# Gates in column tiles, softplus and scan moved, first weights in four pieces from two queues, first norm's squares from a token-major copy of x

## The chip, the cores and the metric

The kernel runs on one core of one Trainium2 chip. The metric is device time in microseconds (us) of one execution, lower is better. A core has TensorE (PE in the profile; PEld is its weight load), VectorE (DVE), ScalarE (ACT), GpSimd (POOL) and SyncE (SP), each with its own queue of instructions, and 16 DMA engines that all transfers share. TensorE writes to PSUM, from which the other engines read.

## The reference

A trunk of two layers over 256 tokens of width 2048, in fp32. Layer 0 runs two recurrences side by side, HGRN2 and RG-LRU; layer 1 is an mLSTM with input and forget gates. Each layer is followed by a gated per-layer embedding (PLE). Cut to what the change touches:

```python
def rmsnorm(x, g):
    return x * lax.rsqrt(jnp.mean(x * x, axis=-1, keepdims=True) + EPS) * g

def rg_lru(xc, w_r, b_r, w_i, b_i, lam):            # layer 0, second half
    r  = sigmoid(blocks(xc) @ w_r + b_r)            # 8 blocks of 128
    ig = sigmoid(blocks(xc) @ w_i + b_i)
    log_a = -8.0 * r * softplus(-lam)
    a = exp(log_a)
    u = sqrt(-expm1(2.0 * log_a)) * (ig * xc)
    return associative_scan(h[t] = a[t] * h[t-1] + u[t])

h = x
for i in range(2):
    hn = rmsnorm(h, norm[i])
    u = hn @ w_in[i]                                # projections of the layer
    ...                                             # mixers
    # layer 1: li = u[gates i] + b_i, lf = log_sigmoid(u[gates f] + b_f), 8 heads each
    h = h + mixed @ w_out[i]
    h = h + rmsnorm(p[i] @ ple_w[i], ple_norm[i]) * silu(h @ ple_gate_w[i])
return rmsnorm(h, final_norm)
```

## The kernel before

**Products.** A fp32 product is made of three matmuls of fp32r halves: a weight is loaded raw (128x1024, 512 KB, five buffers, on SyncE's queue), ScalarE casts it to `whi` (L124, four buffers), VectorE subtracts to get `wlo` (L125, four buffers). Activations are kept as pairs `ahl` of the same kind. `block` multiplies feature-major: 16 matmuls of 128x512 on `whi` (L155), then 16 of 128x256 on `wlo` (L161). `project_tok` multiplies token-major: three matmuls of 128x512 per tile (L196 on `whi`, L197 on `wlo`, L198 on `whi`), in four quarters `kq` of the contraction. `mm3` (L144 to L146) does the same for the small PLE product.

**What sets the order.** Python code issues the instructions in the order of the main line: one projection after another. Beside it run "lanes": generators that yield between steps. `pump()`, called between the two passes of `block` and after the first half of each quarter of `project_tok`, steps every lane once, and what the lanes issue is put behind the last weight instructions of TensorE, ScalarE and VectorE. `drain` runs a lane to its end on the spot. `high_priority` puts an instruction ahead in its engine's queue. Each engine then works strictly through its own row of instructions, so what stands behind a long or a waiting instruction waits too.

**The stages.** First `ple(load_p(0), ...)` multiplies the per-layer embedding: `praw` is loaded and cast (L139), `pw` is loaded, its first half in two pieces of 256 KB. Then `i_proj(0)`, a token-major projection whose quarter `kq` calls `load_x(kq)`: it loads a quarter `xq` of the transposed x, splits it with the gain (L277 on ScalarE, L278 on VectorE), and squares it on ScalarE (L272; the first quarter pair L269); the squares are added up in `acc` on GpSimd and, for the last two pairs, on VectorE (L273). After the fourth quarter the lane "norm" folds `acc` on GpSimd, `rs_tok` sums it over partitions with four small matmul records (L223), `newton` makes the inverse root, and `to_free` (L233 on VectorE, a diagonal `dg`; L236 on TensorE) spreads it over the partitions. The end of `i_proj` scales by `rt`.

Then follow `i_proj(1)`, projections for f and q, the lane "att" (HGRN2; among its matmuls L556, L625 and L643, each of which fills a PSUM bank `mx` that VectorE or ScalarE reads), the projections for `xb` with the convolution `xc` (L738), and the lane "rg", which runs `rg_lru` for the two halves r = 0 and 1: gate matmuls (L704), sigmoids (L708), tanh and exp (L714, L715), squares, `tt` (L721), square root (L723), product (L724), a memset (L725) and the scan (L726, one instruction of 128x1024 on VectorE). They run in the pumps of the two `gate_tok` projections on `ez`. After these, `drain("rg")` runs what is left of the lane, then come four `gate_mul`. PSUM `mx` has three banks.

In layer 1, four token-major projections `ov` are followed by the gates: `gr` is loaded, each half of the contraction gets a zeroed 128x1024 `whi` buffer into which the eight columns of each gate are written as a high and a low half (columns 0, 32, 64 and 96 of each 128), and 32 matmuls (L839) with 128 columns and 256 tokens make the 16 rows. The lane "mix" then runs `gate_stats`: copy the high rows, add the low rows, scale, bias, then logs and two scans; `split8` (L244, L245) splits the running maximum `Mx` in two 8-row tiles and L876 transposes two of the results. `mix(j)`, for four pairs of heads, spreads a row of `Mx` over 128 partitions with `spread`, two matmuls for each head (L252, L253).

**The preparation** `derive` makes the constants of both recurrences on ScalarE and VectorE in the lane "par", among them the softplus of `lam` (L489, L490), all within the first projections.

Of the kernel before, what the change touches and what calls it, by code (L numbers as in the profile page):

```python
# [39 lines left out]
NCST = 128 + 32 + 16 + 2 * 48 + 256  # L40
# [3 lines left out]
def trunk(ctx: ExitStack, tc: tile.TileContext, a, out):  # L44
# [58 lines left out]
    tri2 = cst[:, c0:c0 + 256]  # L103

# [8 lines left out]
    def load_weights(src, pieces=1):  # L113
        parts = []
        for hf in range(2):
# [123 lines left out]
    def split8(x, name):  # L239

        n = x.shape[0]
        hi = tp.tile([8, T], F32R, name=name + "h", tag="s8h", bufs=1)[0:n, :]
        lo = tp.tile([8, T], F32R, name=name + "l", tag="s8l", bufs=1)[0:n, :]
        v.tensor_copy(hi, x)  # L244
        v.tensor_tensor(out=lo, in0=x, in1=hi.bitcast(F32), op=ALU.subtract)  # L245
        return hi, lo

    def spread(o, parts, h):

        n = parts[0].shape[0]  # L250
        w = identr[0:n, h:h + 1].to_broadcast([n, P])
        te.matmul(o, w, parts[0], start=True, stop=False)  # L252
        te.matmul(o, w, parts[1], start=False, stop=True)  # L253
# [48 lines left out]
    def load_p(i):  # L302
        praw = tp.tile([P, 512], F32, name="praw", tag="hn", bufs=3)
        sy.dma_start(out=praw, in_=a["pT"][i])
        return split_act(praw, "p")

    def ple(pact, pool, between):
        pls = []
        for b in range(2):
            parts = load_weights(a["pw"][b], 2 if b == 0 else 1)  # L310
            if b == 1:
                between()
            for j in range(4):
# [150 lines left out]
    def derive():  # L464
        sy.dma_start(out=cst, in_=a["cst"])
# [13 lines left out]

        lam = pall("lam")  # L480
# [14 lines left out]
        v.tensor_scalar(spm8, sp, -8.0, None, op0=ALU.mult)  # L495

# [3 lines left out]
    with m0_scope:  # L500
# [191 lines left out]
        def rg_lru(r, xc):  # L692
# [5 lines left out]
            yield  # L698
            for j in range(2):
# [24 lines left out]
            v.tensor_tensor(out=it, in0=it, in1=tt, op=ALU.mult)  # L724
            v.memset(av.rearrange("p (c t) -> p c t", t=T)[:, :, 0:1], 0.0)  # L725
# [15 lines left out]
        vts = [i_proj(0), i_proj(1)]  # L741
# [44 lines left out]
    v.tensor_copy(identr, ident[0:8, 0:8])  # L786
# [3 lines left out]
    with tc.tile_pool(name="m1", bufs=2) as m1:  # L790
# [35 lines left out]
        for hf in range(2):  # L826
            wt = wp.tile([P, 1024], F32R, name="whi", tag="whi")
# [405 lines left out]
```

## Time and profile before

| | us |
|---|---|
| time, median of 3 runs | 1080.57 (1078.49 to 1080.72) |
| the profiled execution's own time | 1082.2 |
| its span, first to last instruction | 1080.4 |
| PE busy | 1060.6 (98%), 6042 instructions |
| DVE busy | 748.2 (69%), 1087 |
| ACT busy | 579.9 (54%), 852 |
| POOL busy | 131.6 (12%), 103 |
| DMA | 200.26 MB, 185 GB/s in the mean |

The mean granted clock of TensorE is 0.996 of full speed. Row by row, a group line of the profile names a line of the code, an engine, the operation, out<-in with partitions x elements, the count, the busy time and the idle time before it with its releaser. A timeline line has the start, the busy time, the engine, the line, the operation and, in brackets, the idle time before it and what ended it. TensorE's records overlap: a matmul is recorded as busy for longer than the distance to the next start. A full-fp32 matmul (not split) leaves two records.

### The profile page before, as it was taken

Reading aid. Unit: us, or ns where it says so; the run is one execution under the profiler, and the core shown is the slowest. Engines: PE = TensorE matmul, PEld = TensorE weight load, DVE = VectorE, ACT = ScalarE, POOL = GpSimd, SP = SyncE. Lnnn points to the kernel's source line nnn. Section 1 sums busy time; section 2 is a strip of 40 time slices with the busy share of each in tenths; the row PEclk is TensorE's granted clock in tenths of the full one; section 3 lists DMA queues with packets and bytes.
Section 4 is the critical chain, followed back from the end, with each engine's and each line's share of the span. In section 5 each row is a group of like instructions: output and inputs, shape, how many; then the busy total and the mean of one; then the engine's idle time right before and its main releaser. Section 6 shows DMA issues by size and latency. Waiting matters only on the chain.

```text
span 1080.4 us, 15904 instructions
## 1 busy us (share of the span) xinstructions
PE 1060.6 (98%) x6042; PEld 912.9 (84%) x6042; DVE 748.2 (69%) x1087; ACT 579.9 (54%) x852; POOL 131.6 (12%) x103
## 2 busy tenths in 40 slices
PE   7999999999999999999999999999999999999996
PEld 7788888878888888888888888888888888888886
DVE  6958987987777556777544877764456677655665
ACT  7565545857654435556444766554444466434543
POOL 2143542521000000112000000000000005000111
PEclk9999999999999999999999999999999999999999
DMA  8555553533755555555554544445555765554542
GB/s 317 202 205 177 175 186 134 195 131 126 277 197 183 193 195 185 190 189 184 194 195 158 193 156 157 156 166 195 194 190 187 239 217 180 192 191 173 185 176 79
DMA packets 55948, 200.26 MB, mean 185 GB/s; under 512 B 6208, under 2 KB 6464, under 8 KB 55872
## 3 DMA queue, kind: packets, MB, share of 16 engines
q1 hardware_dynamic: 54720, 195.06, 51.5%
q0 software_dynamic: 1152, 4.19, 1.1%
q8 instruction: 47, 0.77, 0.3%
q14 instruction: 29, 0.24, 0.1%
HBM read 197.13 MB, written 2.10 MB: 184 GB/s over the span
## 4 chain that ended last, share of the span: by engine, by line
PE 92%; DVE 4%; ACT 1%; issue 1%; DMA 0%; SPq 0%; DVEq 0%; ACTq 0%
PE mm L155 32%; PE mm L161 17%; PE mm L196 12%; PE mm L197 12%; PE mm L198 12%; DVE wlo L125 2%; DVE ahl L278 1%; PE mm L1082 1%; PE mm L1081 1%; PE mm L1080 1%; PE nu L918 1%; DMA raw<-in_pw_dram 0%; PE mx L444 0%; PE mx L556 0%; ACT whi L124 0%
## 5 line engine op out<-in xcount | busy, mean ns | idle before, releaser
L125 DVE TENSOR_TENSOR wlo<-raw,whi 128x1024 fp32r<-128x1024 f32 (+1 forms) x361 | 455.5, 1286 | 237.1 <-ACT whi L124 136.6
L124 ACT CAST whi<-raw 128x1024 fp32r<-128x1024 f32 (+1 forms) x361 | 377.1, 1048 | 330.3 <-PE mm L155 158.0
L155 PE MATMUL mm<-ahl,whi 128*128 128x512 f32 x1536 | 367.2, 391 | 0.0
L155 PEld LDWEIGHTS mm<-ahl,whi 128*128 128x128 f32 x1536 | 282.1, 188 | 56.1 <-DVE ahl L278 0.7
L196 PE MATMUL mm<-whi,ahl 128*128 128x512 f32 x608 | 239.4, 394 | 0.0
L197 PE MATMUL mm<-wlo,ahl 128*128 128x512 f32 x608 | 236.8, 390 | 1.1 <-DVE wlo L125 1.1
L198 PE MATMUL mm<-whi,ahl 128*128 128x512 f32 x608 | 236.8, 390 | 0.0
L161 PE MATMUL mm<-ahl,wlo 128*128 128x256 f32 x1536 | 202.1, 284 | 0.0
L161 PEld LDWEIGHTS mm<-ahl,wlo 128*128 128x128 f32 x1536 | 195.5, 191 | 6.7
L197 PEld LDWEIGHTS mm<-wlo,ahl 128*128 128x128 f32 x608 | 114.3, 188 | 24.5 <-DVE wlo L125 1.5
L198 PEld LDWEIGHTS mm<-whi,ahl 128*128 128x128 f32 x608 | 114.1, 188 | 23.9
L196 PEld LDWEIGHTS mm<-whi,ahl 128*128 128x128 f32 x608 | 114.3, 188 | 23.4
L167 ACT COPY sm<-mm 128x256 f32<-128x256 f32 x64 | 23.6, 369 | 41.5 <-PE mm L161 41.5
L273 POOL TENSOR_TENSOR acc<-acc,sq 128x512 f32<-128x512 f32 x11 | 17.4, 1580 | 215.4 <-ACT sq L272 215.2
L980 POOL DMA_DIRECT2D row<-in_rows_dram x4 | 2.1, 537 | 285.0 <-DVE u L970 264.9
L168 DVE TENSOR_TENSOR mg<-mm,sm 128x256 f32<-128x256 f32 x64 | 26.6, 415 | 0.1
L803 DVE SCALAR_TENSOR_TENSOR qk<-mg,prm,qk 128x255 f32<-128x255 f32 (+2 forms) x48 | 21.3, 480 | 6.8 <-ACT qk L800 6.5
L1068 POOL TENSOR_TENSOR pl<-pl,row 128x512 f32<-128x512 f32 x6 | 9.2, 1533 | 134.5 <-ACT sq L1052 134.5
L1080 PE MATMUL mm<-whi,ahl 128*128 128x256 f32 x64 | 18.3, 285 | 0.0
L1082 PE MATMUL mm<-whi,ahl 128*128 128x256 f32 x64 | 18.1, 283 | 0.0
L1081 PE MATMUL mm<-wlo,ahl 128*128 128x256 f32 x64 | 18.1, 283 | 0.0
L178 DVE TENSOR_TENSOR mg<-mg,hrs 128x512 f32<-128x512 f32 (+1 forms) x25 | 17.7, 707 | 0.5
(292 smaller groups left out, 825.9 us busy)
## 6 DMA issues: line engine op xcount, KB each, us to landing
raw<-in_ew_dram SPq DMA_DIRECT2D x64, 512.0 KB, 4.3
raw<-in_g_dram SPq DMA_DIRECT2D x56, 512.0 KB, 3.7
raw<-in_eo_dram SPq DMA_DIRECT2D x32, 512.0 KB, 4.0
raw<-in_ov_dram SPq DMA_DIRECT2D x32, 512.0 KB, 3.7
raw<-in_oqk_dram SPq DMA_DIRECT2D x32, 512.0 KB, 4.1
raw<-in_oog_dram SPq DMA_DIRECT2D x32, 512.0 KB, 3.8
raw<-in_oz_dram SPq DMA_DIRECT2D x32, 512.0 KB, 3.8
raw<-in_oo_dram SPq DMA_DIRECT2D x32, 512.0 KB, 3.9
```

The source lines that it names most:

```text
L124: last["act"] = s.copy(h, r).ins
L125: last["dve"] = v.tensor_tensor(out=l, in0=r, in1=h.bitcast(F32), op=ALU.subtract).ins
L155: last["pe"] = te.matmul(ps, parts[k // 8][0][:, c:c + P], act[k // 2][2][:, (k % 2) * 512:(k % 2 + 1) * 512], start=(k == 0), stop=False).ins
L161: last["pe"] = te.matmul(ps[:, T:2 * T], parts[k // 8][1][:, c:c + P], act[k // 2][0][:, k % 2], start=False, stop=(k == KT - 1)).ins
L167: s.copy(small, ps[:, T:2 * T])
L168: v.tensor_tensor(out=dst, in0=ps[:, 0:T], in1=small, op=ALU.add)
L196: te.matmul(ps[hf], xh, wh, start=(k == 0), stop=False)
L197: te.matmul(ps[hf], xh, wl, start=False, stop=False)
L198: last["pe"] = te.matmul(ps[hf], xl, wh, start=False, stop=(k == KT - 1)).ins
L1080: te.matmul(ps[hf], xh, wh, start=(k == 0), stop=False)
L1081: te.matmul(ps[hf], xh, wl, start=False, stop=False)
L1082: last["pe"] = te.matmul(ps[hf], xl, wh, start=False, stop=(k == KT - 1)).ins
```

## The change

Five edits.

1. **First weights.** `load_weights` can alternate between queues, and the first half of the first `pw` is loaded in four pieces of 128 KB, alternating between ScalarE's and SyncE's queue. The cast of `praw` and the PLE matmuls get an explicit place.
2. **First norm.** A token-major copy of x is a new input. Four loads `xt` of 128x1024 are issued on SyncE's queue, two in `load_x(2)` and `load_x(3)`, two behind `i_proj(0)`. Four ScalarE activations square them and sum along the row (`accum_out`), VectorE adds two columns, and the inverse root follows. The eight squares, the adds on GpSimd and VectorE, the fold and the four L223 records of that norm go.
3. **Softplus.** The part of `derive` on `lam` becomes a lane of its own, `decay`, started after `i_proj(0)`, in four pieces. The load of the constants `cst` waits one pump longer.
4. **Scan.** `rg_lru` yields once more before the gate matmuls when r is 1, and once more before the memset and the scan. `drain("rg")` is replaced by stepping the lane until the half that `gate_mul` needs is there.
5. **Gates.** A 128x16x32 tile `wt` holds the gate columns times the gain `on` in fp32. 16 fp32 matmuls (32 columns, 256 tokens) take the raw `hq` and go to four column tiles of one PSUM bank, by k mod 4. ScalarE copies the bank to `gm`, and one fp32 matmul with a constant matrix `gsum` adds the four tiles into 40 rows, one pump later, in `gate_stats`, which then reads PSUM directly. `split_rows` puts both halves of `Mx` into one 40-row tile, and `spread` is one matmul per head.

```diff
-                sy.dma_start(out=r, in_=src[:, hf * 1024 + c:hf * 1024 + c + n])
+                queues[(hf * 1024 + c) // n % len(queues)].dma_start(out=r, in_=src[:, hf * 1024 + c:hf * 1024 + c + n])
...
+    def split_rows(x):
+
+        both = tp.tile([40, T], F32R, name="s8", tag="s8", bufs=1)
+        v.memset(both.bitcast(F32), 0.0)
+        v.tensor_copy(both[0:8], x)
+        v.tensor_tensor(out=both[32:40], in0=x, in1=both[0:8].bitcast(F32), op=ALU.subtract)
+        return both
+
+    def spread(o, both, h):
+
+        te.matmul(o, identr[:, h:h + 1].to_broadcast([40, P]), both, start=True, stop=True)
...
-            parts = load_weights(a["pw"][b], 2 if b == 0 else 1)
+            parts = load_weights(a["pw"][b], *((4, (s, sy)) if b == 0 else ()))
...
+    def load_xt(i):
+        sy.dma_start(out=xt[i], in_=a["x"][i // 2 * P:(i // 2 + 1) * P, i % 2 * 1024:(i % 2 + 1) * 1024])
+
+    def x_norm():
+
+        for i in range(4):
+            s.activation(xt[i], xt[i], AF.Square, accum_out=xss[:, i % 2, i // 2:i // 2 + 1])
+            if i < 3:
+                yield
+        y = xss[:, 0]
+        v.tensor_tensor(out=y, in0=y, in1=xss[:, 1], op=ALU.add)
+        v.tensor_scalar(y, y, 1.0 / D, EPS, op0=ALU.mult, op1=ALU.add)
+        yield from spread_norm(rsqrt_cols(y), 0)
...
             acth.append(gained(pair_of(xq, j), "en", j))
-            add_square(gp if j < 6 else v, acc, pair_of(xq, j), j == 0)
-        if i == 3:
-            start("norm", finish_norm([folded(acc)], 0))
+        if i >= 2:
+            load_xt(i - 2)
+        if i == 2:
+            start("norm", x_norm())
...
             yield
+            if r:
+                yield
             for j in range(2):
                 for w, (dst, bias) in enumerate(((av, "bbr"), (it, "bbi"))):
...
             v.tensor_tensor(out=it, in0=it, in1=tt, op=ALU.mult)
+            yield
             v.memset(av.rearrange("p (c t) -> p c t", t=T)[:, :, 0:1], 0.0)
             v.tensor_tensor_scan(tt, av, it, 0.0, op0=ALU.mult, op1=ALU.add)
...
-        vts = [i_proj(0), i_proj(1)]
+        vts = [i_proj(0)]
+        start("par", decay())
+        vts.append(i_proj(1))
...
-        drain("rg")
         for j in range(4):
             if j == 2:
                 drain("att")
+            if j % 2 == 0:
+                while ("h", j // 2) not in res:
+                    step("rg")
...
+        wt = m1.tile([P, KT, 32], F32, name="wt", tag="wt", bufs=1)
+        gp.memset(wt, 0.0)
+        v.tensor_tensor(out=wt[:, :, 0:16], in0=gr, in1=pall("on").unsqueeze(2).to_broadcast([P, KT, 16]), op=ALU.mult)
         ps = pm.tile([P, 512], F32, name="mm", tag="mm")
...
+        for k in range(KT):
+            c = 32 * (k % 4)
+            te.matmul(ps[c:c + 32, 0:T], wt[:, k], pair_of(hq, k // 2)[:, (k % 2) * T:(k % 2 + 1) * T],
+                      start=(k < 4), stop=(k >= KT - 4))
+        gm = m1.tile([P, T], F32, name="gm", bufs=1)
+        s.copy(gm, ps[:, 0:T])
...
+        def gate_stats():
+            yield
+            ps = px.tile([P, 512], F32, name="mx", tag="mx")
+            te.matmul(ps[0:40, 0:T], gsum, gm, start=True, stop=True)
...
-                s.copy(x, ps[c:c + 8, 0:T])
-                v.tensor_tensor(out=x, in0=x, in1=ps[64 + c:72 + c, 0:T], op=ALU.add)
-                v.tensor_tensor(out=x, in0=x, in1=norm["rs"][0:8], op=ALU.mult)
+                v.tensor_tensor(out=x, in0=ps[c:c + 8, 0:T], in1=norm["rs"][c:c + 8], op=ALU.mult)
```

Lines of the kernel after lie a little lower: L124 and L125 become L126 and L127, L155 and L161 become L157 and L163, L196 to L198 become L198 to L200, L236 becomes L238, L643 becomes L671, L704 becomes L737, L726 becomes L760, L839 becomes L872.

On ScalarE, at the start of the program, the row of instructions was this; `raw` and `whi` are the first PLE weights, `praw` the embedding, `pl` the product.

```order
L139 ACT_TABLE_LOAD
L139 CAST ahl<-praw 128x2x256
L124 CAST whi<-raw 128x512 x2
L124 CAST whi<-raw 128x1024 x2
L324 COPY pl<-mm 128x512
```

And now:

```order
L124 DMA raw<-in_pw_dram 128x256 x2
L126 ACT_TABLE_LOAD
L126 CAST whi<-raw 128x256
L141 CAST ahl<-praw 128x2x256
L126 CAST whi<-raw 128x256 x3
L126 CAST whi<-raw 128x1024 x2
L326 COPY pl<-mm 128x512
```

Two loads are issued ahead of everything, the first weight piece is cast ahead of the embedding, and there are four casts of half the width.

On VectorE, around the r = 0 scan during the first `ez` projection, the row before was this; `xc` is the convolution, `f` and `A` belong to HGRN2, the two wide ones on `tt` and `it` to RG-LRU (the scan is printed under the name of another operation).

```order
L125 TENSOR_TENSOR wlo<-raw,whi 128x1024 x2
L738 SCALAR_TENSOR_TENSOR xc<-mg,prm,xc 128x255 x2
L738 SCALAR_TENSOR_TENSOR xc<-mg,prm,xc 128x254 x2
L738 SCALAR_TENSOR_TENSOR xc<-mg,prm,xc 128x253 x2
L726 SCALAR_TENSOR_TENSOR tt<-av,it 128x1024
L631 TENSOR_TENSOR f<-f,tot_2480 128x8x64
L125 TENSOR_TENSOR wlo<-raw,whi 128x1024
L638 COPY A<-mx 64x8x64
L125 TENSOR_TENSOR wlo<-raw,whi 128x1024
L716 TENSOR_TENSOR it<-it,xc 128x1024
L125 TENSOR_TENSOR wlo<-raw,whi 128x1024 x2
```

And now:

```order
L127 TENSOR_TENSOR wlo<-raw,whi 128x1024 x2
L772 SCALAR_TENSOR_TENSOR xc<-mg,prm,xc 128x255 x2
L772 SCALAR_TENSOR_TENSOR xc<-mg,prm,xc 128x254 x2
L772 SCALAR_TENSOR_TENSOR xc<-mg,prm,xc 128x253 x2
L127 TENSOR_TENSOR wlo<-raw,whi 128x1024
L659 TENSOR_TENSOR f<-f,tot_2470 128x8x64
L127 TENSOR_TENSOR wlo<-raw,whi 128x1024
L666 COPY A<-mx 64x8x64
L760 SCALAR_TENSOR_TENSOR tt<-av,it 128x1024
L127 TENSOR_TENSOR wlo<-raw,whi 128x1024 x2
L480 SCALAR_TENSOR_TENSOR u<-u,mm 128x512
```

The scan (L726, now L760) moved from ahead of `f` and the copy to `A` to behind both, and the product `it` with `xc` of the half r = 1 (L716) no longer stands here.

On TensorE, around the gates of layer 1, between the last `ov` projection and the first blocks of `oqk`, the row was this; `li`, `Bc` and the `Mx` halves are results of `gate_stats`.

```order
L198 MATMUL mm<-whi,ahl 128x512
L839 MATMUL mm<-ahl,whi 128x256 x32
L155 MATMUL mm<-ahl,whi 128x512 x16
...
L876 MATMUL mx<-cst,li 128x8 x2
L876 MATMUL mx<-cst,Bc 128x8 x2
...
L252 MATMUL mx<-Mxh,identr 128x256
L253 MATMUL mx<-Mxl,identr 128x256
L252 MATMUL mx<-Mxh,identr 128x256
L253 MATMUL mx<-Mxl,identr 128x256
```

And now:

```order
L200 MATMUL mm<-whi,ahl 128x512
L872 MATMUL mm<-hq,wt 32x256 x16
L157 MATMUL mm<-ahl,whi 128x512 x16
...
L888 MATMUL mx<-gm,cst 40x256
...
L912 MATMUL mx<-cst,li 128x8 x2
L912 MATMUL mx<-cst,Bc 128x8 x2
L251 MATMUL mx<-s_5769,identr 128x256 x2
```

16 matmuls of 32 columns stand for 32 of 128, one matmul for the sum is added one pass later, and the two spread matmuls now follow directly on the transposes.

More of the change, by code (lines that the diff above doesn't have):

```diff
@@ L39 @@
 NPRM = _o
[L40 removed]
+NCST = 128 + 32 + 16 + 2 * 48 + 256 + 40
 @with_exitstack
@@ L103, in trunk @@
     tri2 = cst[:, c0:c0 + 256]
+    c0 += 256
+    gsum = cst[:, c0:c0 + 40]
     def pc(name, i=0, n=None):
@@ L110, in pall, with load_weights @@
         return pc(name, 0, PRM[name][1])
-    def load_weights(src, pieces=1):
+    def load_weights(src, pieces=1, queues=(sy,)):
         parts = []
@@ L237, in to_free @@
         return st[:, 0:T]
[L239 to L253, printed above, removed]
+    def split_rows(x):
[6 more added lines that the diff above has]
+        te.matmul(o, identr[:, h:h + 1].to_broadcast([40, P]), both, start=True, stop=True)
     def folded(acc, *more):
@@ L304, in load_p @@
         sy.dma_start(out=praw, in_=a["pT"][i])
-        return split_act(praw, "p")
+        with tc.high_priority(offset=0 if i else 800):
+            return split_act(praw, "p")
     def ple(pact, pool, between):
@@ L319, in ple @@
                         c = ((j % 2) * 4 + jj * 2 + k) * P
-                        mm3(ps[:, jj * T:(jj + 1) * T], hi[:, c:c + P], lo[:, c:c + P], pact, k, k == 0, k == 1)
+                        with ExitStack() as behind:
+                            if "pe" in last:
+                                behind.enter_context(tc.issue_after(last["pe"]))
+                            mm3(ps[:, jj * T:(jj + 1) * T], hi[:, c:c + P], lo[:, c:c + P], pact, k, k == 0, k == 1)
                 if j % 2:
@@ L401, in trunk @@
     pls = ple(load_p(0), p0, lambda: sy.dma_start(out=prm, in_=a["prm"]))
-    identr = cp.tile([8, 8], F32R, name="identr")
-    acc = cp.tile([P, 512], F32, name="acc", tag="acc")
+    identr = cp.tile([40, 8], F32R, name="identr")
     acth = []
+    xt = [hp.tile([P, 1024], F32, name="xt", tag="h") for _ in range(4)]
+    xss = cp.tile([P, 2, 2], F32, name="xss")
+    def load_xt(i):
[9 more added lines that the diff above has]
+        yield from spread_norm(rsqrt_cols(y), 0)
     def load_x(i):
@@ L423, in finish_norm, with spread_norm @@
             yield
-        norm["rt"] = rs_tok(accs)
+        yield from spread_norm(rs_tok(accs), lag)
+    def spread_norm(rt, lag):
+        norm["rt"] = rt
         yield
@@ L478, in derive, with decay @@
         yield
+    def decay():
         lam = pall("lam")
@@ L650, in i_proj @@
             ps = project_tok(a["ei"], g, acth, None if g else load_x)
-            vt = hp.tile([P, 1024], F32, name="vt", tag="h")
+            if g == 0:
+                for i in (2, 3):
+                    load_xt(i)
             while "rt" not in norm:
                 step("norm")
+            vt = hp.tile([P, 1024], F32, name="vt", tag="h")
             for hf in range(2):
@@ L783, in trunk @@
     l0.close()
-    v.tensor_copy(identr, ident[0:8, 0:8])
+    v.memset(identr.bitcast(F32), 0.0)
+    for c in (0, 32):
+        v.tensor_copy(identr[c:c + 8], ident[0:8, 0:8])
     norm.clear()
@@ L824, in trunk @@
         sy.dma_start(out=gr, in_=a["ogf"])
+        wt = m1.tile([P, KT, 32], F32, name="wt", tag="wt", bufs=1)
+        gp.memset(wt, 0.0)
+        v.tensor_tensor(out=wt[:, :, 0:16], in0=gr, in1=pall("on").unsqueeze(2).to_broadcast([P, KT, 16]), op=ALU.mult)
         ps = pm.tile([P, 512], F32, name="mm", tag="mm")
-        for hf in range(2):
-            wt = wp.tile([P, 1024], F32R, name="whi", tag="whi")
-            gp.memset(wt.bitcast(F32), 0.0)
-            w3 = wt.rearrange("p (k c) -> p k c", c=P)
-            f3 = wt.bitcast(F32).rearrange("p (k c) -> p k c", c=P)
-            for w in range(2):
-                src = gr[:, hf * 8:(hf + 1) * 8, w * 8:(w + 1) * 8]
-                c = w * 32
-                s.copy(w3[:, :, c:c + 8], src)
-                v.tensor_tensor(out=w3[:, :, 64 + c:72 + c], in0=src, in1=f3[:, :, c:c + 8], op=ALU.subtract)
-            for kk in range(8):
-                k = hf * 8 + kk
-                for i, x in enumerate(acth[k // 2][0:2]):
-                    te.matmul(ps[:, 0:T], wt[:, kk * P:(kk + 1) * P], x[:, k % 2],
-                              start=(k == i == 0), stop=(k == KT - 1 and i == 1))
+        for k in range(KT):
[4 more added lines that the diff above has]
+        s.copy(gm, ps[:, 0:T])
         def t8(name):
@@ L877, in gate_stats @@
             v.tensor_copy(aT, px_[:, 0:32])
-        start("mix", gate_stats(ps))
+        start("mix", gate_stats())
         SC = 0.25 * 128.0 ** -0.5
@@ L1159, in _const @@
     c[:, o:o + P] = np.where(si <= np.arange(P)[None, :], 0.0, -1e30)
+    o += 256
+    for h in range(8):
+        c[:, o + h] = si[:, 0] % 32 == h
+        c[:, o + 32 + h] = si[:, 0] % 32 == 8 + h
     return c
```

9 lines of the change are left out of this document (7 added, 2 removed).

## The prediction

> **What bounds the kernel now.** I read the first part of the page, then its chain, then the waits of the matmul engine, then windows of the places that the waits name.
>
> ```profile
> PE 1060.6 (98%) x6042; PEld 912.9 (84%) x6042; DVE 748.2 (69%) x1087; ACT 579.9 (54%) x852; POOL 131.6 (12%) x103
> ...
> PE 92%; DVE 4%; ACT 1%; issue 1%; DMA 0%; SPq 0%; DVEq 0%; ACTq 0%
> ```
>
> TensorE is busy in 1060.6 us, 98% of the span, and holds 92% of the chain. So a step counts only if it shortens TensorE's own work, its idle time, or its time at a low clock. The idle time has few owners:
>
> ```profile
> PE mm L144 <- ACT whi L124: 6.8, 2, 5.6
> PE mx L643 <- DVE A L638: 2.0, 1, 2.0
> PE mm L197 <- DVE wlo L125: 1.1, 1, 1.1
> PE st L236 <- DVE dg L233: 0.8, 1, 0.8
> ```
>
> Columns are the total, the number of waits and the longest. These four lines are all of TensorE's waits on other engines: 10.7 us. The windows give each engine's busy time, the granted clock, the DMA share and GB/s:
>
> ```profile
> 7.62:13.50 5.88, 5.88 (x27) 5.88 (x28) 3.99 (x6) 3.83 (x5) 0.00 (x0) 1.00 1.01 388
> 13.50:21.69 8.19, 8.19 (x69) 8.19 (x68) 6.83 (x9) 7.16 (x14) 1.58 (x1) 1.00 1.03 411
> 21.69:28.50 6.81, 6.81 (x32) 5.64 (x31) 6.81 (x8) 6.81 (x13) 4.71 (x4) 1.00 0.71 273
> 235.80:238.80 3.00, 0.99 (x8) 0.82 (x8) 2.59 (x4) 2.99 (x5) 0.00 (x0) 1.00 0.22 74
> 238.80:242.20 3.40, 3.40 (x13) 2.78 (x11) 0.67 (x1) 2.63 (x7) 0.00 (x0) 0.54 0.65 231
> ```
>
> Two things hide in them. From 7.62 to 13.50 TensorE is full, with 27 matmuls: 0.218 us each. From 13.50 on the same matmuls take 8.19/69 = 0.119. So it starts at half speed, though the clock column, which has no record there, says 1.00. And behind the wait of 2.0 us the clock is 0.54 for 3.4 us. Nearly all other work runs dense (issue holds 1% of the chain). The places to cost are therefore the start, the first norm, the scan and, because it is TensorE's own work, the gates.
>
> **The start.** Before, ScalarE casts the activation and then the first pieces:
>
> ```profile
> 3.44 0.62 ACT L139 CAST ahl<-praw 128x512 fp32r<-128x512 f32 x1 [1.43 <-DMA praw<-in_pT_dram]
> 4.94 0.62 ACT L124 CAST whi<-raw 128x512 fp32r<-128x512 f32 x1 [0.88 <-DMA raw<-in_pw_dram]
> ...
> 5.61 0.58 PE L144 MATMUL mm<-ahl,whi 128*128 128x256 f32 x1 [5.61 <-ACT whi L124]
> ...
> 7.62 0.58 PE L144 MATMUL mm<-ahl,whi 128*128 128x256 f32 x1 [1.21 <-ACT whi L124]
> ```
>
> The first weight piece (256 KB) is cast 1.50 after the activation's cast, the first matmul follows 0.05 after the cast's end, and the second piece comes 2.0 later. The change halves the pieces to 128 KB and issues half of them from ScalarE's queue. At half of 1.50 the first cast starts at 4.2; at some 0.4 for a cast of half the width, the first matmul is at 4.6 (bounds 4.2, if both queues share well, and 5.4, if nothing but the cast shrinks). The next piece follows after 1.0 instead of 2.0, at about 5.6, so the dense run starts 2.0 earlier. Six matmuls wait in each piece, 1.3 us at 0.218, so they cover the following piece of 131 KB, 0.34 at 388 GB/s. If the dense run must last as long as before (5.9) until the full clock comes, everything moves 2.0 to 2.2: I take **2.1**. If the clock comes at 13.50 whatever starts earlier, 2.0/0.218 = 9 matmuls move out of the full-speed part at 0.119 each: 1.1. If it comes a 3.4 window earlier, another 3.4/0.218 = 16 matmuls save 0.099 each: 2.6. Issuing from ScalarE costs nothing that counts: it idles 1.43 before 3.44. Bounds 1.0 to 2.6.
>
> **The first norm.** Before, x's squares are summed on GpSimd and VectorE from the transposed x.
>
> ```profile
> 28.52 0.39 PE L196 MATMUL mm<-whi,ahl 128*128 128x512 f32 x1
> 29.98 0.50 PE L197 MATMUL mm<-wlo,ahl 128*128 128x512 f32 x1 [1.07 <-DVE wlo L125]
> ...
> 42.13 0.50 PE L223 MATMUL st<-ones,acc 128*128 128x1 f32 x4
> ...
> 47.61 0.39 PE L197 MATMUL mm<-wlo,ahl 128*128 128x512 f32 x1
> 47.84 0.39 PE L198 MATMUL mm<-whi,ahl 128*128 128x512 f32 x1
> 49.07 0.70 PE L236 MATMUL st<-dg,ones 128*128 128x256 f32 x2 [0.84 <-DVE dg L233]
> ```
>
> Dense matmuls of this form start 0.23 apart (47.61, 47.84), so L197's wait costs 29.98 − 28.52 − 0.23 = 1.23. It comes from VectorE, which is 6.81 of 6.81 busy there (window 21.69) beside GpSimd with 4.71. The change takes the sums off both; VectorE keeps only two tiny adds. I take **1.2** (0 if VectorE stays late for other reasons). The four L223 records leave TensorE: **0.3** of their 0.50. L236 starts 1.0 late because its diagonal, the last link of the norm, is late; the norm now starts from four squares on ScalarE, which need no sums on two other engines after them, so I take **1.0** (0 if the token-major x is late). Each square of 128x1024 takes at most twice the 0.62 of the 128x512 cast, and the four replace eight of half the size: nothing on ScalarE. What it costs is DMA: 2.1 MB of new loads, 1.3 us per 512 KB at 411 GB/s. Two of them stand ahead of i_proj(0)'s later weights, and the queue is full until about 24 us. Rival A prices that; in the forecast the five raw buffers hide it.
>
> **The scan.** VectorE and TensorE before, and a visit of the same L704 form at full clock for comparison:
>
> ```profile
> 233.15 2.28 DVE L726 TENSOR_TENSOR_SCAN tt<-av,it 128x1024 f32<-128x1024 f32 x1
> 235.35 0.66 DVE L631 TENSOR_TENSOR f<-f,tot 128x512 f32<-128x512 f32 x1
> 235.94 1.22 DVE L125 TENSOR_TENSOR wlo<-raw,whi 128x1024 fp32r<-128x1024 f32 x1
> 237.18 0.68 DVE L638 COPY A<-mx 64x512 f32<-64x512 f32 x1
> ...
> 235.61 0.39 PE L198 MATMUL mm<-whi,ahl 128*128 128x512 f32 x1
> 238.01 1.13 PE L643 MATMUL mx<-f,k 128*128 128x128 f32 x8 [2.01 <-DVE A L638]
> 238.98 3.52 PE L704 MATMUL mx<-xc,bw 128*128 128x256 f32 x8
> 241.94 0.84 PE L196 MATMUL mm<-whi,ahl 128*128 128x512 f32 x1
> ...
> 208.09 1.89 PE L704 MATMUL mx<-xc,bw 128*128 128x256 f32 x8
> 209.64 1.55 PE L161 MATMUL mm<-ahl,wlo 128*128 128x256 f32 x10
> ```
>
> L643 waits for VectorE's copy, which stands behind the scan. The loss has three pieces: 238.01 − 235.61 − 0.23 = 2.17 idle; L704 takes 2.96 instead of 1.55, 1.41 by the low clock; the next matmul is busy 0.84 instead of 0.39, 0.45. Together **4.0**. In the new order the scan stands behind f, wlo and the copy. With the r = 1 gate matmuls moved to the next projection, L643's PSUM bank is no longer one that the copy reads, and it needs only f: 233.15 + 1.22 + 0.66 = 235.0, ahead of 235.84 when TensorE arrives. If it still needed the copy (235.0 + 1.22 + 0.68 = 236.9), 1.1 of waiting would stay, without the low clock. The scan now delays later wlo by 2.28; four wlo buffers cover that. Bounds 1.5 to 4.2.
>
> The Trainium skill ("TensorE: Matmul & The Clock Gate", HAM oscillation) says that a gap costs clock only from about 3.4 us up; by that the cure would be worth 2.2 and the sum 1.8 less. The trace disagrees: one gap of 2.2 us, then 0.54.
>
> **The gates.**
>
> ```profile
> 588.03 4.00 PE L839 MATMUL mm<-ahl,whi 128*128 128x256 f32 x32
> 591.86 1.32 PE L155 MATMUL mm<-ahl,whi 128*128 128x512 f32 x5
> ...
> 123.39 0.89 PE L556 MATMUL mx<-q,k 128*32 128x48 f32 x64
> 124.21 0.98 PE L161 MATMUL mm<-ahl,wlo 128*128 128x256 f32 x6
> ...
> 619.05 0.38 PE L252 MATMUL mx<-Mxh,identr 8*128 8x256 f32 x1
> ...
> 619.70 2.17 PE L161 MATMUL mm<-ahl,wlo 128*128 128x256 f32 x16
> ```
>
> Removed: 32 matmuls, 3.83 us. Added: 16 full-fp32 matmuls of 32 columns, each recorded twice like L704's (4 instructions, 8 records, 0.194 per record): 32 records. L556 has the same kind of tile: 64 records in 0.82, so fours share the array. 0.051 per four of 48 columns would be 0.27 for 256 columns; L704's record says 0.194. Eight fours are 1.6 to 2.2; I take 1.9, a gain of **1.9**. The one summing matmul (40x256, two records and its entry) costs **0.6**, and the spreads, 0.65 per visit of two heads now, halve their records: four visits save some 0.23 each, **0.9**. ScalarE loses four copies and VectorE four splits: no gain, both have slack. VectorE's product for wt waits for a DMA issued as before, with one wlo behind it that TensorE needs some 4 us later: nothing.
>
> Sum: 2.1 + 1.2 + 0.3 + 1.0 + 4.0 + 1.9 − 0.6 + 0.9 = 10.8. Against it new waits: the statistics that give the spread rows now start one pump later, and a spread waits if they are not ready (0 to 1.5); and one r = 1 gate matmul in ez depends on ScalarE by a thin margin. I take 0.8. Net 10.0. The profiled execution took 1082.2, so 1072.2; it lies 1.6 above the median 1080.57, so **1070.6**. From this kernel's three runs, 0.2% (2.2 us) is about what a measurement can tell from no change.
>
> **The rivals.**
>
> A: the token-major loads collide with the start. For it: the DMA share is 1.03 until 21.69. Against: it falls to 0.71 from there. If the two early loads push the weights by 2.6 with no slack, and the 2.1 of the start is lost to the same queue: 4.7 less, 1075.3; with all four, 1077.8.
>
> B: the column tiles do not share the array. 32 records at 0.194 are 6.2 instead of 1.9: 4.3 less, 1074.9. Against it stands L556. The Trainium skill (the same page, The mechanism, under row/col tiling) says that a weight load overlaps running matmuls only where the row group differs, and column tiles share theirs; L556's 64 records in 0.82 do not look like it.
>
> C, slower: ScalarE becomes the bound in the ez stage. The moved gates interleave sigmoid, tanh and sqrt with the casts and add three table loads:
>
> ```profile
> 243.40 1.28 ACT L715 ACT_TABLE_LOAD   x1
> 244.69 0.51 ACT L715 ACTIVATE av<-av,spm 128x256 f32<-128x256 f32 x1
> ...
> 242.20:280.00 37.80, 37.80 (x185) 31.83 (x185) 29.98 (x45) 29.75 (x54) 4.94 (x3) 1.00 0.50 177
> ```
>
> 29.75 of 37.8 busy; 3 × 1.28 = 3.85 makes 33.6, room on average, but the casts come in pairs. Each cast pair late enough for a gap like the scan's costs 4.0 (2.2 idle, 1.9 clock). Three undo the 10 and more: 1082.6; one gives 1074.6. The Trainium skill ("ScalarE: Activation LUTs", What ACT_TABLE_LOAD costs) adds a drain of 1.38 us to each load, which would be 8.0 in place of 3.85 and fill the window's slack; here the next activation starts 0.01 after the load.
>
> D: the change does not do what it says. The scan still stands in the way, or the clock still falls, and 2.5 of the 4.0 stays; or VectorE is still late in i_proj: 1073 to 1074.
>
> **Chances.** Forecast 0.66, A 0.14, B 0.07, D 0.08, C 0.05 (with part of C still faster, since one late pair leaves a gain). The range: all upper bounds (start 2.6, no new waits, scan 4.2, gates at 0.194) give 1.9 more, 1068.7, and the spread of the runs another 1.7: 1067. Upwards it takes in A with two loads, B and D: 1077. Faster by over 0.2% 0.93, within 0.03, slower 0.04.
>
> **What would show it.** Right: the first matmul near 4.6 and i_proj's first near 19.6; no waits at L199, L238 or L671; clock 1.00 from 235 to 243; column-tile records in fours, the gate visit near 1.9. Wrong: waits of i_proj on raw (A), a gate visit of 6 (B), TensorE waiting on whi in ez (C), a new wait at the spread over 1.5.

## The result, and the profile after

The changed kernel takes 1072.16 us (median; before 1079.53): ratio 0.9928, 95% interval 0.9912 to 0.9944. A second set gave 1072.67 against 1081.09, 0.9918 (0.9904 to 0.9933). The forecast was 1070.6. The profile below is from the second set, since the profiled execution of the first ran TensorE at less than a third of its speed throughout and took 3759.18 us. The profile's own time is 1072.67; the forecast for the profiled execution was 1072.2.

The head of the page and the chain of the changed kernel:

```profile
span 1070.9 us, 15869 instructions
PE 1055.4 (99%) x6032; PEld 907.1 (85%) x6032; DVE 740.0 (69%) x1085; ACT 581.8 (54%) x852; POOL 123.1 (11%) x96
...
PE 95%; DVE 2%; ACT 1%; issue 1%; DMA 0%; DVEq 0%; ACTq 0%
```

TensorE is busy for 5.2 us less (part of that is time at a low clock), and the span is 9.5 shorter: the rest is idle time that went. Its waits on other engines:

```profile
PE mm L146 <- ACT ahl L141: 5.2, 1, 5.2
PE mx L671 <- DVE f L659: 0.9, 1, 0.9
```

Four owners have become two, 6.1 us instead of 10.7. The waits of L199 and L238 are gone; one at L671 has taken the place of L643's, and it is for `f`, not for the copy.

To see where time went, I follow one matmul: the n-th of the 4896 large ones, in before and after. The step of the difference at each place is the gain there. Against the shown profile of before it is 2.0 at the first projection, 3.0 over the first norm (1.24 + 0.12 at L199, 0.37 + 0.12 at the sums, 1.12 at L238), 6.3 around the scan with 3.7 given back where the moved gate matmuls now stand, and 2.1 at the gates. Together 9.7; 0.2 is lost behind the last of these matmuls, which leaves the 9.5, near the 10.0 that were forecast for this pair of executions.

The gates and the spread in the changed kernel:

```profile
580.50 1.93 PE L872 MATMUL mm<-hq,wt 128*32 128x256 f32 x32
582.36 0.96 PE L157 MATMUL mm<-ahl,whi 128*128 128x512 f32 x3
...
591.78 0.63 PE L888 MATMUL mx<-gm,cst 128*40 128x256 f32 x2
592.33 1.34 PE L163 MATMUL mm<-ahl,wlo 128*128 128x256 f32 x9
...
610.21 0.49 PE L251 MATMUL mx<-s,identr 40*128 40x256 f32 x2
610.64 1.57 PE L163 MATMUL mm<-ahl,wlo 128*128 128x256 f32 x11
```

582.36 − 580.50 = 1.86 us for the gates, where 3.83 stood; the sum takes 0.55 to the next start, a visit of two spreads 0.43.

The moved r = 1 gate matmuls in the `ez` projections, and the busy time of all engines there:

```profile
239.25 1.03 PE L737 MATMUL mx<-xc,bw 128*128 128x256 f32 x4
241.32 1.13 PE L737 MATMUL mx<-xc,bw 128*128 128x256 f32 x4
246.62 1.89 PE L737 MATMUL mx<-xc,bw 128*128 128x256 f32 x8
...
235.00:262.00 27.00, 27.00 (x137) 22.84 (x136) 14.84 (x29) 24.31 (x51) 3.10 (x3) 1.00 0.45 153
```

TensorE is busy in all 27.00 us, with ScalarE at 24.31: the added table loads fill ScalarE but stop nobody.

### The profile page after: what moved, and what is told of

It is laid out like the page before. It is cut to its first block, busy times and chain, and to the rows that moved or that the text cites. A ratio compares the mean times of both kernels' runs of the same rounds, so it can differ in the third digit from the quotient of the medians.

```text
span 3757.4 us, 15869 instructions
## 1 busy us (share of the span) xinstructions
PE 3742.9 (100%) x6032; PEld 2344.5 (62%) x6032; DVE 732.4 (19%) x1085; ACT 592.6 (16%) x852; POOL 90.5 (2%) x96
## 4 chain that ended last, share of the span: by engine, by line
PE 100%; DVE 0%; DMA 0%; ACT 0%; DVEq 0%; issue 0%
PE mm L157 34%; PE mm L163 17%; PE mm L199 13%; PE mm L198 13%; PE mm L200 13%; PE nu L954 1%; PE mm L1118 1%; PE mx L737 1%; PE mm L1117 1%; PE mm L1116 1%; PE mx L465 1%; PE mx L584 0%; PE mm L147 0%; PE mx L697 0%; PE mm L1031 0%; PE mx L1076 0%
## 5 line engine op out<-in xcount | busy, mean ns | idle before, releaser
L157 PE MATMUL mm<-ahl,whi 128*128 128x512 f32 x1536 | 1285.9, 1095 | 0.0
L157 PEld LDWEIGHTS mm<-ahl,whi 128*128 128x128 f32 x1536 | 670.3, 446 | 518.0 <-issue 516.8
L127 DVE TENSOR_TENSOR wlo<-raw,whi 128x1024 fp32r<-128x1024 f32 (+1 forms) x363 | 445.6, 1228 | 2351.8 <-ACT whi L126 1159.6
L126 ACT CAST whi<-raw 128x1024 fp32r<-128x1024 f32 (+1 forms) x363 | 377.0, 1039 | 2370.3 <-PE mm L157 1121.6
L163 PEld LDWEIGHTS mm<-ahl,wlo 128*128 128x128 f32 x1536 | 640.1, 521 | 69.0 <-issue 64.3
L198 PE MATMUL mm<-whi,ahl 128*128 128x512 f32 x608 | 671.8, 1105 | 0.0
L199 PE MATMUL mm<-wlo,ahl 128*128 128x512 f32 x608 | 666.0, 1095 | 0.0
L200 PE MATMUL mm<-whi,ahl 128*128 128x512 f32 x608 | 664.8, 1093 | 0.0
L163 PE MATMUL mm<-ahl,wlo 128*128 128x256 f32 x1536 | 661.6, 675 | 0.0
L199 PEld LDWEIGHTS mm<-wlo,ahl 128*128 128x128 f32 x608 | 263.5, 433 | 230.8 <-issue 226.9
L200 PEld LDWEIGHTS mm<-whi,ahl 128*128 128x128 f32 x608 | 259.3, 427 | 235.7 <-issue 235.3
L198 PEld LDWEIGHTS mm<-whi,ahl 128*128 128x128 f32 x608 | 259.9, 427 | 233.6 <-issue 230.4
L1116 PE MATMUL mm<-whi,ahl 128*128 128x256 f32 x64 | 44.5, 695 | 0.0
L1118 PE MATMUL mm<-whi,ahl 128*128 128x256 f32 x64 | 44.4, 694 | 0.0
L1116 PEld LDWEIGHTS mm<-whi,ahl 128*128 128x128 f32 x64 | 36.3, 568 | 1.1 <-issue 1.1
L1117 PEld LDWEIGHTS mm<-wlo,ahl 128*128 128x128 f32 x64 | 36.3, 566 | 0.4 <-issue 0.4
L1118 PEld LDWEIGHTS mm<-whi,ahl 128*128 128x128 f32 x64 | 36.2, 566 | 0.0
L954 PE MATMUL nu<-vt,scw 128*128 128x257 f32 x32 | 28.8, 1137 | 0.0
L737 PE MATMUL mx<-xc,bw 128*128 128x256 f32 x32 | 27.6, 1089 | 0.0
```

What stands on the lines that cost most here:

```text
L126: last["act"] = s.copy(h, r).ins
L127: last["dve"] = v.tensor_tensor(out=l, in0=r, in1=h.bitcast(F32), op=ALU.subtract).ins
L157: last["pe"] = te.matmul(ps, parts[k // 8][0][:, c:c + P], act[k // 2][2][:, (k % 2) * 512:(k % 2 + 1) * 512], start=(k == 0), stop=False).ins
L163: last["pe"] = te.matmul(ps[:, T:2 * T], parts[k // 8][1][:, c:c + P], act[k // 2][0][:, k % 2], start=False, stop=(k == KT - 1)).ins
L198: te.matmul(ps[hf], xh, wh, start=(k == 0), stop=False)
L199: te.matmul(ps[hf], xh, wl, start=False, stop=False)
```

## The experiments

**The changed kernel again** (no edit), for the profile above.

> The changed kernel again, for a profile at full clock. All theories expect the measured gain of 7 to 8 us, against 10.0 in the sum. Theory T (a term is too large): no new wait of TensorE above 0.3 us shows, and one of the four places is worth less than its term, most likely the start, whose lower bound of 1.1 instead of 2.1 explains 1.0, and the VectorE wait in i_proj(0), 1.2. Rival W (a new wait): the places give their 10.8, and waits of TensorE of 2 to 3 us in total stand at the spread of layer 1 or in the ez projections.

1072.67 us, four runs within 0.3. Neither theory holds whole: a term was too large (the scan), and one new wait of 0.9 stands. It lies in the first `ez` projection, where the rival looked, but it is a third of the rival's size, and it is L671's for `f`.

**The gates alone**, on the kernel before.

```diff
+            c = 32 * (k % 4)
+            te.matmul(ps[c:c + 32, 0:T], wt[:, k], pair_of(hq, k // 2)[:, (k % 2) * T:(k % 2 + 1) * T],
+                      start=(k < 4), stop=(k >= KT - 4))
...
+        te.matmul(o, identr[:, h:h + 1].to_broadcast([40, P]), both, start=True, stop=True)
```

> The kernel before with the gates part alone (column tiles, one summing matmul, one spread matmul per head). Theory T: 2.2 us faster, with the gate visit on TensorE at 1.9 instead of 3.83 and no wait at the spread. Rival W: the visit is 1.9 too, but 1 to 1.5 of it is lost in a wait at the first spread, so 0.7 to 1.2 faster. Column tiles that run one after another: visit of 6 us, 2 us slower.

1077.93, ratio 0.9971 (0.9960 to 0.9982): 3.1 us, 1.9 to 4.3. In its trace the steps at the gates, the sum and the spreads are the same as in the changed kernel, 2.1 together, with no wait at a spread. Theory T holds; the 1.0 by which the median gained more lies within the interval.

**The scan alone.**

```diff
+            if r:
+                yield
...
             v.tensor_tensor(out=it, in0=it, in1=tt, op=ALU.mult)
+            yield
...
-        drain("rg")
+            if j % 2 == 0:
+                while ("h", j // 2) not in res:
+                    step("rg")
```

> The kernel before with the moved gates and scan of RG-LRU alone. Theory T: 4.0 us faster, clock 1.00 between 230 and 245 us, no wait of 2.0. Rival W: the wait and the low clock go, but ScalarE or VectorE are late later in the ez projections, so 1 to 2.5 us faster with new waits of TensorE on whi or wlo there.

1078.77, ratio 0.9976 (0.9966 to 0.9986): 2.6 us, 1.5 to 3.7, short of the 4.0. No wait on `whi` or `wlo` appears in `ez`, so the rival's mechanism is wrong too. The trace shows L643 waiting 0.9 for `f`, as in the whole change.

**The start alone.**

```diff
-            parts = load_weights(a["pw"][b], 2 if b == 0 else 1)
+            parts = load_weights(a["pw"][b], *((4, (s, sy)) if b == 0 else ()))
...
```

The edit also gives the cast of `praw` and the PLE matmuls their explicit place.

> The kernel before with the first weights in four pieces from two queues alone. Theory T with the full term: first matmul near 4.6, i_proj's first matmul near 19.6 instead of 21.69, 2.1 us faster. Lower bound: the full clock comes at 13.5 again, i_proj starts near 20.6, 1.1 us faster. Rival W: the start comes 2 earlier and is given back in i_proj(0), whose weights are then late: 0 to 0.5 faster.

1079.58, ratio 0.9988 (0.9979 to 0.9998): 1.3 us, 0.2 to 2.3. The first matmul is at 5.18, i_proj at 19.36. That would be 2.3 against the shown profile, but the two kernels above, whose start is that of before, have i_proj at 19.58 and 19.64. So the shown profile of before had an unusually late start, and the next experiment asks why. L197's wait is gone in this trace too, but most of it comes back at the norm's diagonal, where the wait grows from 0.8 to 1.7: one addition of the squares on GpSimd is recorded with 6.97 us, where the shown profile has 1.29 to 1.88.

**The kernel before, once more** (no edit).

> The kernel before, unchanged, profiled once more. Theory L (the shown profile had a late clock): i_proj's first matmul comes near 19.6 in this one, as in the two kernels whose start was not edited, and the full clock near 10 to 11 us; or, if this execution is late again, the clock at 13 to 14 and i_proj near 21.7. Rival F (the start is fixed by the code): 21.69 again and the clock at 13.8, whatever the execution.

1077.97 us, 4.2 less than the profiled execution that was shown, from the same instructions. Windows of 3.41 us, cut at the changes of the granted clock: first the shown execution of before, then this one.

```profile
6.97:10.38 3.41, 2.76 (x13) 2.76 (x14) 1.50 (x2) 2.29 (x3) 0.00 (x0) 1.00 1.01 392
10.38:13.79 3.41, 3.41 (x18) 3.41 (x18) 2.80 (x5) 2.34 (x4) 0.00 (x0) 1.00 1.00 384
235.66:239.07 3.41, 1.40 (x11) 1.09 (x10) 3.00 (x4) 3.40 (x6) 0.00 (x0) 1.00 0.27 91
239.07:242.49 3.42, 3.42 (x10) 2.71 (x9) 0.40 (x1) 2.36 (x6) 0.00 (x0) 0.50 0.60 214
```

```profile
6.32:9.73 3.41, 3.41 (x18) 3.41 (x18) 1.43 (x2) 1.76 (x2) 0.00 (x0) 1.00 0.97 327
231.60:235.01 3.41, 1.80 (x8) 1.14 (x7) 3.38 (x4) 2.10 (x3) 0.00 (x0) 1.00 0.02 8
235.01:238.42 3.41, 3.02 (x18) 2.79 (x19) 1.47 (x2) 3.41 (x9) 0.00 (x0) 1.00 0.59 174
```

The first matmuls of this execution:

```profile
5.15 0.58 PE L144 MATMUL mm<-ahl,whi 128*128 128x256 f32 x1 [5.15 <-ACT whi L124]
...
5.85 0.58 PE L144 MATMUL mm<-ahl,whi 128*128 128x256 f32 x1
```

The second of these lines is the first matmul on the second weight piece. It starts at 5.85 without a wait; in the shown execution it started at 7.62, behind a wait of 1.21 for a piece that had landed late. From 3.5 to 5.5 us the DMA engines moved 119 to 197 GB/s there and 287 to 393 here; why is not shown.

The full clock comes at the end of a window that TensorE fills: at 13.79 in the shown execution, whose window before was busy for only 2.76 of 3.41 because of that wait, and at 9.73 here. (Below the full clock the column still says 1.00 at the start, since no record lies there.) And the gap of 2.17 us at the scan, the same in both, fell whole into one window there (1.40 busy) and cost the clock for the next; here a boundary cut it (1.80 busy), and the clock stayed. i_proj starts at 18.91 instead of 21.69, 2.8: 1.8 by the weights, which land earlier, and 1.0 by the clock. The clock at the scan is the other 1.7; the two make up the 4.2 but for 0.3 that the norm gives back. Theory L holds for the clock, but the start of before differs first by when its weights land. Of 53 timed runs of before in the three later sets, 32 have a mean clock of 0.996, like the shown one, with a median of 1081.8; the other 21, at 0.997 or 0.998, lie at 1078.5 to 1081.0. The mean tells that there was a low window, not where; that it was the scan's is seen in the traces alone.

**The first norm alone.**

```diff
-            add_square(gp if j < 6 else v, acc, pair_of(xq, j), j == 0)
-        if i == 3:
-            start("norm", finish_norm([folded(acc)], 0))
+        if i >= 2:
+            load_xt(i - 2)
+        if i == 2:
+            start("norm", x_norm())
```

> The kernel before with the first norm from the token-major copy alone. Forecast's terms: the wait of i_proj(0) on VectorE (1.2), the small matmuls (0.3) and the wait for the diagonal (1.0) go: 2.5 faster. Rival A (the loads collide): these go, but i_proj(0) waits for its weights, 0 to 1 faster.

1075.46, ratio 0.9950 (0.9931 to 0.9968): 5.4 us, 3.5 to 7.5, more than forecast. Its waits:

```profile
PE mm L144 <- ACT whi L124: 5.7, 2, 5.3
PE mx L662 <- DVE A L657: 2.0, 1, 2.0
```

The waits of L197 and L236 are gone, no matmul of i_proj(0) waits for a weight, and the steps in the trace are the 3.0 of the whole change. Rival A falls. How GpSimd made L197 late is seen in the splits of x on VectorE (fastest, median and slowest in ns), first in the shown profile of before, then here:

```profile
L278 DVE SCALAR_TENSOR_TENSOR ahl<-xq,prm,ahl x16: 468/475/1580, 14.5 to 38.0; 128x256 fp32r<-128x256 f32 x16
L278 DVE SCALAR_TENSOR_TENSOR ahl<-xq,prm,ahl x16: 435/478/485, 13.6 to 29.3; 128x256 fp32r<-128x256 f32 x16
```

In before, the five splits that run beside an addition on GpSimd (L273) take 1.51 to 1.58 us, and each ends 0.28 behind the end of an addition; the other eleven take 0.47 or 0.48, and none of the sixteen here takes over 0.49. So the additions cost VectorE some 5 us, though they ran on another engine. With the start alone it was the other way round: the addition of 6.97 us ran beside splits of 0.47.

The other 2.4 are not in this place: all four runs kept a mean clock of 0.998, so none paid for the scan's gap, which stands 3 us earlier against the clock's windows. That the shift causes this is likely, and was not tried. Against the second trace of before, which kept its clock too, the profiled execution gains 2.8.

**f ahead of the convolution**, on the changed kernel.

```diff
-                v.tensor_tensor(out=qv, in0=qv, in1=tv[:, :, 0:1].to_broadcast([P, n, B]), op=ALU.mult)
+                with tc.high_priority(offset=600 if B == 64 and g else 0):
+                    v.tensor_tensor(out=qv, in0=qv, in1=tv[:, :, 0:1].to_broadcast([P, n, B]), op=ALU.mult)
```

> The changed kernel, with the product f of the second head group put ahead of the convolution on VectorE. If L671's gap is the wait for f and nothing else: the wait of 0.9 goes and the kernel is 1.0 faster than the changed one, near 1071.6. If L671 waits for the copy to A as well (its PSUM bank): the same wait under another name, 1072.7 again.

1071.18 (1071.03 to 1071.93), ratio to before 0.9911 (0.9889 to 0.9934). VectorE and TensorE in the changed kernel:

```profile
228.18 1.21 DVE L127 TENSOR_TENSOR wlo<-raw,whi 128x1024 fp32r<-128x1024 f32 x1
229.31 0.68 DVE L659 TENSOR_TENSOR f<-f,tot 128x512 f32<-128x512 f32 x1
...
228.88 0.39 PE L200 MATMUL mm<-whi,ahl 128*128 128x512 f32 x1
230.13 1.13 PE L671 MATMUL mx<-f,k 128*128 128x128 f32 x8 [0.86 <-DVE f L659]
231.02 0.48 PE L198 MATMUL mm<-whi,ahl 128*128 128x512 f32 x1
```

And with f first:

```profile
225.37 0.68 DVE L660 TENSOR_TENSOR f<-f,tot 128x512 f32<-128x512 f32 x1
...
230.69 0.68 DVE L667 COPY A<-mx 64x512 f32<-64x512 f32 x1
...
228.44 0.39 PE L200 MATMUL mm<-whi,ahl 128*128 128x512 f32 x1
228.67 1.05 PE L672 MATMUL mx<-f,k 128*128 128x128 f32 x8
229.48 0.48 PE L198 MATMUL mm<-whi,ahl 128*128 128x512 f32 x1
```

f ends at 226.05, and the matmul starts 0.23 behind the last one instead of 1.25. The copy still ends only at 231.37, so L671 does not wait for it. The step in the trace is 1.1. By the runs this version is faster than before; against the changed kernel the intervals of the two ratios overlap (0.9904 to 0.9933 there), so there the gain rests on the trace.

**Unread matmuls ahead of the first weights**, on the changed kernel.

```diff
+    warm = pst.tile([P, 512], F32, name="st", tag="st")
+    for _ in range(5):
+        te.matmul(warm[:, 0:T], ones[:, 0:P], ones, start=True, stop=True)
```

> The changed kernel with five matmuls on a constant tile ahead of the first weights, whose result nobody reads. Theory L (full clock comes at the end of the first window of some 3.4 us in which TensorE works throughout): full clock between 5.2 and 8.5, some 15 to 25 matmuls of the start at 0.11 instead of 0.22, so 1.5 to 2.7 faster, near 1070.5. Rival D (from there the start is bound by the weights' arrival): clock early, i_proj starts less than 0.7 earlier, 0 to 0.7 faster.

1072.14, ratio to before 0.9918 (0.9900 to 0.9936), the ratio of the changed kernel in the second set. The clock is full at 4.25 instead of 11.06, but i_proj starts only 0.4 earlier (19.28), and the traces of f first and of the single tile below, with this start and no unread matmuls, have it at 19.24 and 19.26. TensorE now waits for the halves of weights and activation, 0.8 + 0.6 + 0.3 us. Rival D: from there the start is bound by what arrives.

**The same on the kernel before.** The edit is the same three lines.

> The kernel before, with the five unread matmuls at the start alone. Theory L (the slow executions of before are those whose full clock comes a window late): the clock is full by 4.3 in every execution, so i_proj starts near 19 in all of them, the runs above 1081.5 vanish, and the median is 1.0 to 2.5 faster than before's. Rival: the start of before is bound by the arrival of its weights in most executions, and what spreads its runs is the clock behind the scan's gap alone; then the median is within 0.5.

1079.38, ratio 0.9984 (0.9973 to 0.9996): 1.7 us, 0.4 to 2.9, and no run above 1080.3 where before reaches 1083.5. So the unread matmuls are worth something here, as Theory L had it. But in the trace i_proj starts at 20.50, not near 19, and the clock did not stay full:

```profile
4.87:8.28 3.41, 1.43 (x10) 1.04 (x9) 1.38 (x3) 0.87 (x3) 0.00 (x0) 1.00 0.85 288
8.28:11.70 3.42, 3.42 (x18) 3.42 (x18) 1.26 (x2) 2.63 (x4) 0.00 (x0) 0.50 1.03 412
233.56:236.97 3.41, 1.50 (x11) 1.48 (x12) 2.96 (x3) 3.40 (x7) 0.00 (x0) 1.00 0.40 144
236.97:240.40 3.43, 3.43 (x17) 2.90 (x16) 0.85 (x1) 3.41 (x8) 0.00 (x0) 1.00 0.53 165
```

In this execution the second piece made TensorE wait 1.98 us; the gap lies in one window, 1.43 busy, and the next is at half clock. No trace of the change's four pieces has such a gap. At the scan a window that was busy for 1.50 kept the clock. TensorE comes to the old norm 1.6 later than in the second trace of before and waits less there: behind the diagonal the two stand at 46.90 and 46.82. So where the 1.7 come from is not shown.

**All gate matmuls in one column tile**, on the changed kernel.

```diff
-            c = 32 * (k % 4)
+            c = 0
...
-                      start=(k < 4), stop=(k >= KT - 4))
+                      start=(k == 0), stop=(k == KT - 1))
...
-            te.matmul(ps[0:40, 0:T], gsum, gm, start=True, stop=True)
+            te.matmul(ps[0:40, 0:T], gsum[0:32], gm[0:32], start=True, stop=True)
```

> The changed kernel with all sixteen gate matmuls in one column tile, one after another (they add up in PSUM, so the summing matmul has one tile to read). If column tiles share the array, this visit takes 32 records of 0.19 to 0.22: 6.2 to 6.9 us instead of 1.96, and the kernel is 4.3 to 4.9 slower than the changed one. If the gain came from the smaller weights alone, the visit stays near 2 us.

1077.40, ratio to before 0.9971 (0.9959 to 0.9982): 4.7 more than the changed kernel of the second set, and 5.2 more at this place in the traces. The visit in this trace:

```profile
580.11 7.09 PE L872 MATMUL mm<-hq,wt 128*32 128x256 f32 x32
587.13 3.92 PE L157 MATMUL mm<-ahl,whi 128*128 128x512 f32 x16
```

7.02 us for the same 32 records that take 1.86 in four tiles: 3.8 times. The tiles share the array, and the gain is theirs, not the narrow weights'.

**The softplus alone.**

```diff
-        vts = [i_proj(0), i_proj(1)]
+        vts = [i_proj(0)]
+        start("par", decay())
+        vts.append(i_proj(1))
...
```

As in the change, the load of `cst` waits one pump longer too.

> The kernel before with the softplus lane moved alone. Forecast: nothing that counts, within 1 us of before, since TensorE's waits in i_proj(0) are on a later VectorE chain than this one. Rival: VectorE's work of the softplus is what makes L197's wlo or the norm's diagonal late, and 1 to 2 us go with it.

1079.02, ratio 0.9979 (0.9967 to 0.9992): 2.3 us, 0.9 to 3.6. TensorE's waits:

```profile
PE mm L144 <- ACT whi L124: 6.6, 1, 6.6
PE mx L650 <- DVE A L645: 2.0, 1, 2.0
PE mm L197 <- DVE wlo L125: 0.3, 1, 0.3
```

The wait for the norm's diagonal is gone and L197's is 0.3 instead of 1.1, with the first norm untouched. For the diagonal the rival holds: in before, the softplus steps run on VectorE from 40.33 to 47.51, among the norm's own, and the norm's first step starts 3.4 behind the last L223; here it starts 2.2 behind it, and the softplus follows later. L197's wait is another matter. It ends at 29.98 in before, ten us ahead of the first softplus step on VectorE, so these steps cannot cause it. Here VectorE's row has another order in i_proj(0), with one split of x instead of two ahead of the `wlo` that L197 needs; which part of the edit does that is not shown.

**f first and the unread matmuls.** Both edits.

> The changed kernel with f ahead of the convolution and the five unread matmuls at the start. If the two add up: 1.5 and 0.5 faster than the changed one, near 1070.7. If the start is bound by the weights' arrival in both: 1071.1, the same as with f first alone.

1071.11 (1071.08 to 1071.20), ratio to before 0.9912 (0.9894 to 0.9930): f first alone again. i_proj starts at 19.13, with f first alone at 19.24: the second theory holds.

## Why the prediction held, and which steps did not

**The sum for the pair of profiles** came out at 9.5 us against 10.0 forecast, the time of the profiled execution at 1072.67 against 1072.2. **The step that failed is the last:** "it lies 1.6 above the median 1080.57, so 1070.6". The 1.6 was no offset that both kernels share. It was that one execution's own start and clock: its second weight piece late by 1.8, its full clock a window later, and the clock halved at the scan. The sum had already counted these as gains: 4.2 of the 9.5 are what the same instructions gave in another execution of before. The changed kernel has no gap that long, its runs at full speed lie within 1 us, and its profiled execution is its median. That 1072.2 is so near is in part luck: the scan's term was 1.3 too large, the norm's 0.5 too small, and the 0.8 kept for new waits made up for most of the rest.

**The start (2.1).** The step in the trace is 2.0, but before makes 2.8 with no edit, when its second piece lands early. Alone the edit is worth 1.3 of the median. The first cast came at 4.25 as forecast, the first matmul at 5.23 instead of 4.6: the activation's cast now stands behind the first piece's, 0.61 more, and the matmul needs both. This order could be read beforehand. i_proj starts at 19.68 even so, near the 19.6 of the forecast; it varies with the clock's windows, and the same start gave 19.24 where the full clock came at 10.14 instead of 11.06.

**The first norm (2.5).** 3.0, and the waits named are gone. L197's was read rightly as VectorE beside GpSimd. But the sum has no term for the softplus, which alone removes most of the same waits and gives 1.5 of the 3.0 in its trace: the diagonal was late by the softplus steps too, not by the squares alone. The gains of the five parts alone, 1.3 + 5.4 + 2.3 + 2.6 + 3.1 = 14.7, exceed the 8.9 of the whole. These 1.5 are counted twice in them. The rest is not located; each interval is 2 to 4 us wide, and a part alone can also shift the scan's gap against the clock's windows.

**The scan (4.0).** 2.66 against the shown profile (6.3 less 3.7), 1.0 against the second one of before. Two errors. The 1.9 of low clock were taken as due to the gap whenever it comes, but the second execution had the gap and kept the clock; by the mean clock, some 6 of 10 executions lose it. And "235.0, ahead of 235.84 when TensorE arrives": the same edit takes the L704 visit away ahead of it (1.65 in the trace), so TensorE arrives at 234.2 by the forecast's own numbers, 0.8 before f. The measured wait is 0.86. The sentence of the Trainium skill ("TensorE: Matmul & The Clock Gate", HAM oscillation) that a gap costs clock only from some 3.4 us up is not what these traces show: 2.0 and 2.2 us were enough where they fell into one window. Another sentence of that page of the Trainium skill (What's actually happening) says that the window runs freely and that the transition depends on where the first matmul lands in it. The traces agree: the changes lie whole multiples of 3.41 us apart.

**The gates (2.2) and new waits (0.8).** 2.1, term by term: the tiles 1.75 (1.9 forecast), the sum 0.76 (0.6), the transposes and spreads 1.1 (0.9). No wait came at the spread, and none of the gate matmuls in `ez` waited for ScalarE; the wait that came, L671's in the first `ez` projection, was not among the new waits.

**The rivals.** A: the loads of the token-major x cost nothing that shows; TensorE waits for no weight in i_proj(0). B: the single tile shows what it would have cost, 5.2 in its place. C: 24.31 of 27.00 on ScalarE, no wait. D came in part, as a wait for f.

**Still open:** why the norm alone gains 2.4 more than its place shows. Against the execution of before that kept its clock it gains 2.8, which points to the executions of before that lose the clock or start late. That the edit itself keeps the clock, by where it puts the gap in the windows, no run tried.

## What to carry to other kernels

Before a profile's waits for first loads and its clock effects are priced, look at several executions: what the same instructions give in another execution is no gain of the change, and an execution's distance from its median goes only once into a sum. When an edit removes work ahead of a meeting of two engines, work out anew when each arrives. Two edits that clear the same engine's row do not add.

## What the runs showed of the hardware

A window of 3.41 us in which TensorE was busy for 1.40, 1.41, 1.43 or 1.47 us was followed by one at half clock; with 1.50 and 1.80 the clock stayed. The 1.47 is near the end of the single-tile kernel, the 1.41 the scan's gap with the start alone:

```profile
232.25:235.67 3.42, 1.41 (x7) 0.90 (x6) 3.06 (x4) 2.67 (x4) 0.00 (x0) 1.00 0.04 11
235.67:239.09 3.42, 3.42 (x13) 3.06 (x13) 1.23 (x1) 2.51 (x7) 0.00 (x0) 0.50 0.66 216
```

To come up, the clock asked for more: 2.76 busy of 3.41 did not bring it, 2.99 did with f first and the unread matmuls, and 3.15 in the changed kernel with unread matmuls, whose clock is full from the end of this window on:

```profile
0.84:4.25 3.41, 3.15 (x7) 2.52 (x8) 0.03 (x1) 1.29 (x2) 1.13 (x3) 1.00 0.60 179
```

So in these traces a window had to be nearly full to leave the low clock, and less than half full was enough to keep the full one.
